# Two products of an MLP as seven quadrant products instead of eight, on one Trainium2 core

## The chip, the cores and the metric

The program runs on one core of one Trainium2 chip. The core has five engines with a queue of instructions each: TensorE (PE in the profile; its weight loads are listed as PEld), VectorE (DVE), ScalarE (ACT), GpSimd (POOL) and SyncE (SP), which here only issues DMAs. Each engine works through its queue in program order; semaphores make one engine wait for another. The metric is the time of one execution in microseconds of device time; lower is better. The kernel before takes 1270.71 us (median of 3 runs, 1268.05 to 1270.95).

## The reference

One layer of an encoder for 1024 prompt tokens and 32 sample tokens, model width 1024, in fp32. The change touches only the MLP at its end (`D_FF` is 4096):

```python
def trunk_layer(x, c, s0, ...):
    ...
    x = layer_norm(DN_ALPHA * x + (1.0 + gate1) * (mix @ w_o + b_o), ln1_g, ln1_b)
    h2 = x * (1.0 + scale2) + shift2
    f = jnp.square(jax.nn.relu(h2 @ w_up + b_up)) @ w_down + b_down
    x = layer_norm(DN_ALPHA * x + (1.0 + gate2) * f, ln2_g, ln2_b)
    return x, s_fin, v_rows
```

## The kernel before

**Tokens and precision.** The 1056 tokens stand in three blocks (`BLK`): blocks 0 and 1 have 384 tokens, block 2 has 288 (256 prompt, 32 sample). Activations are kept feature-major, 128 features by the tokens of a block. Every fp32 product is made from split operands: a value is a high part rounded to fp32r (a copy on ScalarE) and a low part (value minus high part, on VectorE, or on POOL for the activations), and three passes are multiplied, high by high, high by low, low by high (`PASS`). So one output tile of 128 features, summed over 1024 inputs, is 8 k-tiles by 3 passes, 24 matmuls.

**Weights.** `Units` (L146) takes the weights as units of 128 x 1024 (512 KB) in the order of their use, `main_units`: SP loads up to five ahead into `wst`, and two halves each are split into `whl` (L139 on ScalarE, L140 on VectorE), three units ahead. The list runs through all phases of the program without a break.

**Phase C/D.** After the mixers comes the output projection of each block (`out_proj`, matmuls at L251), the first layer norm on token-major rows (`norm1`: transposes at L1005 and L229, statistics, then h2 split by ScalarE and POOL, L238 and L241), and the MLP. For the layer norm the rows of x are loaded again (`xr`, L1021) with the gain row `ging` (L1013) and multiplied (`x_rows`, L1028 on VectorE for block 0, L1030 on ScalarE and L1031 on POOL for the others).

**The MLP** goes through the 32 feature tiles of f in eight groups of four. `up` (L251 for its matmuls) makes one tile for all three blocks: 24 matmuls per block, then relu with the bias (L1070, ScalarE), the square (L1071, VectorE), and the split of f (L1072, L1073). `down` (L1096) takes one weight unit, a pair of output tiles, and sums over the four tiles of the group: 12 matmuls per output tile and block, and adds them with the gate to the accumulator `acc` in SBUF (L1101). In the loop of `main_d`, the down pairs of group g and the up tiles of group g+1 alternate. The last group's down product is taken in pieces of tokens (`down_last`, L1159), each followed by the second layer norm of its rows (`norm2`).

**What sets the order.** The generators are woven by `Order`, which emits TensorE's work of the main stream and puts the other streams' pieces between by estimated times; the order of each engine's queue is the order of emission. PSUM has eight banks for output tiles in this phase (`mm()`).

Of the kernel before, what the change touches and what calls it, by code (L numbers as in the profile page):

```python
# [19 lines left out]
P = 128  # L20
# [16 lines left out]
# columns of the packed per-feature vectors  # L37
# [8 lines left out]
# weight units, each [128, 1024]  # L46
# [51 lines left out]
def build(tc, io):  # L98
# [4 lines left out]
    with ctx:  # L103
# [4 lines left out]
        wp = ctx.enter_context(tc.tile_pool(name="wp", bufs=1))  # L108
# [33 lines left out]
        class Units:  # L142
            """Weight units in the order of their use: loaded and split ahead of it."""

            def __init__(self, us):
                self.us, self.raw, self.hl, self.i = us, [], [], 0  # L146
                self.last, self.split = None, {}

            def ahead(self, nl, ns):
                while len(self.raw) < min(nl, len(self.us)) or len(self.hl) < min(ns, len(self.us)):  # L150
# [4 lines left out]
                    else:  # L155
                        if self.last and len(self.hl) == len(self.us) - 1:
                            hl = self.last()
                        else:
                            hl = wp.tile([P, 2, 1088], F32R, tag="whl", name="whl", bufs=3)
# [3 lines left out]
            def get(self, u, n=1):  # L163
                """the next n units, split; every use of the earlier ones has been emitted"""
# [60 lines left out]
        def turn(tiles, b, k):  # L225
            """token-major tiles of a block -> [128 features of tile k, tokens] in PSUM"""
# [5 lines left out]
        def split_affine(dst, pt, k, b, av, cv, tmp):  # L232
            """dst (hi, lo) = av * pt + cv"""
# [10 lines left out]
        PASS = ((0, 0), (0, 1), (1, 0))  # L244

        def fm_mm(pt, hl, act, n, korder, done):
            """[128 out features, n tokens]; hl holds 8 k-tiles of [128, 128]"""
            ks = list(korder)
            for i, k in enumerate(ks):
                for j, (a, b_) in enumerate(PASS):  # L250
                    PE.matmul(pt[:, :n], hl[:, a, 128 * k:128 * k + 128], act[:, b_, k, :n],  # L251
                              start=(i == 0 and j == 0), stop=(i == 7 and j == 2))
# [10 lines left out]
        def stack_s(pool, tag, bufs, wide=1):  # L263
            """the sample tokens, hi and lo rows side by side"""
# [4 lines left out]
        def tm_part(pt, hls, act, off, n, width, ks, passes=PASS):  # L269
            """[n tokens, width]; hls are the units that hold the k-tiles in order"""  # L270
# [22 lines left out]
        def proj_act(u0, ms, func, pool, tag, alloc=mm, ready=None):  # L293
            for m in ms:
                hl = wu.get(u0 + m)
                for b in range(3):
# [4 lines left out]
                    def done(pt):  # L301
# [8 lines left out]
        # ================= phase A: input layer norm, gMLP =================  # L310
        main_units = ([U_ZU + m for m in range(4)] + [U_R + m for m in range(4)]
                      + [U_V, U_V + 1, U_K, U_Q, U_K + 1, U_Q + 1, U_V + 2, U_V + 3]
                      + [U_O + m for m in range(8)] * 3 + [U_UP + m for m in range(4)])
        for g in range(7):
            main_units += [U_DN + 4 * g, U_UP + 4 * g + 4, U_DN + 4 * g + 1, U_UP + 4 * g + 5,
                           U_DN + 4 * g + 2, U_DN + 4 * g + 3, U_UP + 4 * g + 6, U_UP + 4 * g + 7]
        main_units += [U_DN + 28 + dp for dp in range(4)]
# [675 lines left out]
        with tc.tile_pool(name="pd", bufs=1, reuse_waits="tile") as pd, \  # L993
# [86 lines left out]
            def up(m, fs):  # L1080
                hl = wu.get(U_UP + m)
                f = new_f()
                for b in range(3):
                    yield from up_tile(hl, m, f, b)
# [222 lines left out]
```

## Time and profile before

| what | value |
|---|---|
| median of 3 runs | 1270.71 us (1268.05 to 1270.95) |
| span of the profiled execution | 1268.7 us |
| TensorE busy | 1217.2 us, 96% |
| VectorE busy | 728.5 us, 57% |
| ScalarE busy | 439.7 us, 35% |
| POOL busy | 246.6 us, 19% |
| moved from and to HBM | 94.29 MB read, 4.65 MB written |

The profile is of one execution; the page gives its span, from the first to the last instruction. It is 2.0 us under the median of the runs, and inside their spread. "Busy" of TensorE counts pipelined matmuls. A row of the grouped views reads: line, engine, operation, tiles written and read, shapes, count, then total busy time and the mean in ns of one, then the engine's idle time just before such instructions and what ended it. In a timeline or a chain, a row begins with its start and its length in us. Line numbers in rows of the profile before are those of the kernel printed above; those of the changed kernel are named as such.

### The profile page before, as it was taken

To read this page: it belongs to the slowest core of one execution; us is meant where nothing else is said; L and a number is where in the kernel's file an instruction comes from. 1 tells how busy PE (TensorE), PEld (TensorE's weight loads), DVE (VectorE), ACT (ScalarE), POOL (GpSimd) and SP (SyncE) were. 2 spreads that over 40 slices of the span, in tenths; PEclk is the share of its full clock that TensorE was granted. 3 is DMA by queue.
4 is the path that set the end of the run, shared out by engine and by line. 5 is a ranking of instruction groups with operands and counts; after the bars stand their busy time and mean duration, and the time that the engine had idled before them with its cause. 6 is when DMAs were issued, how large, how long until landed. Compare 5 with 4: busy or idle time off the path is not lost.

```text
span 1268.7 us, 21648 instructions
## 1 busy us (share of the span) xinstructions
PE 1217.2 (96%) x8779; PEld 1166.3 (92%) x8779; DVE 728.5 (57%) x1654; ACT 439.7 (35%) x960; POOL 246.6 (19%) x435
## 2 busy tenths in 40 slices
PE   5999996999899999999999999999999999999996
PEld 3689996988788899999999999999999999999996
DVE  5763999578886789644334434443344344344467
ACT  4463322445566666622122122221222221212311
POOL 3441232345584235200000000000000000000034
PEclk9999998899899999999999999999999999999998
DMA  9503555110002633020111111101111111111112
GB/s 373 205 2 130 177 221 183 34 35 19 22 35 72 236 134 117 9 75 36 49 50 51 34 51 50 51 34 51 51 50 34 50 51 49 36 51 50 67 38 100
DMA packets 29396, 100.34 MB, mean 79 GB/s; under 512 B 3408, under 2 KB 4912, under 8 KB 29296
## 3 DMA queue, kind: packets, MB, share of 16 engines
q1 hardware_dynamic: 29296, 98.95, 22.1%
q8 instruction: 69, 1.13, 0.4%
q14 instruction: 31, 0.25, 0.1%
HBM read 94.29 MB, written 4.65 MB: 78 GB/s over the span
## 4 chain that ended last, share of the span: by engine, by line
PE 81%; DVE 10%; DMA 4%; ACT 2%; issue 2%; POOL 1%; SPq 0%; DVEq 0%; ACTq 0%
PE mm L251 40%; PE mm L1096 26%; PE mm L1159 3%; PE zp L285 2%; DMA wst<-in_w_dram 2%; DVE jk L888 2%; PE mm L285 2%; DVE whl L140 1%; DVE wad L888 1%; PE mm L229 1%; PE zp L251 1%; DMA wad<-in_w_dram 1%; PE mm L1005 1%; PE gt L768 1%; DVE zx L746 1%
## 5 line engine op out<-in xcount | busy, mean ns | idle before, releaser
L251 PE MATMUL mm<-h,whl 128*128 128x384 f32 (+1 forms) x2304 | 377.1, 322 | 0.0
L251 PEld LDWEIGHTS mm<-h,whl 128*128 128x128 f32 x2304 | 370.7, 188 | 0.3
L1096 PE MATMUL mm<-f,whl 128*128 128x384 f32 (+1 forms) x2016 | 328.9, 323 | 0.0
L1096 PEld LDWEIGHTS mm<-f,whl 128*128 128x128 f32 x2016 | 326.7, 188 | 0.0
L139 ACT CAST whl<-wst 128x512 fp32r<-128x512 f32 x202 | 115.0, 618 | 283.0 <-PE mm L1096 203.9
L1101 DVE SCALAR_TENSOR_TENSOR acc<-mm,G,acc 128x384 f32<-128x384 f32 (+1 forms) x224 | 105.0, 490 | 168.6 <-PE mm L1096 168.6
L1071 DVE TENSOR_TENSOR rl<-rl 128x384 f32<-128x384 f32 (+1 forms) x96 | 50.7, 528 | 193.7 <-ACT rl L1070 193.7
L140 DVE TENSOR_TENSOR whl<-wst,whl 128x512 fp32r<-128x512 f32 x202 | 147.6, 766 | 17.0 <-ACT whl L139 14.3
L219 POOL TENSOR_SCALAR rs<-mv 128x1 f32<-128x1 f32 (+1 forms) x27 | 7.7, 285 | 756.0 <-DVE mv L218 756.0
L251 PE MATMUL mm<-hT,whl 128*128 128x384 f32 (+1 forms) x792 | 129.6, 322 | 1.0 <-ACT mix L307 1.0
L251 PEld LDWEIGHTS mm<-hT,whl 128*128 128x128 f32 x792 | 127.0, 188 | 2.6 <-ACT mix L307 1.6
L1070 ACT ACTIVATE rl<-mm,pv 128x384 f32<-128x384 f32 (+1 forms) x96 | 53.3, 555 | 202.0 <-PE mm L251 202.0
L251 PE MATMUL mm<-mhl,whl 128*128 128x384 f32 (+1 forms) x576 | 100.7, 329 | 3.0 <-DVE whl L140 3.0
L251 PEld LDWEIGHTS mm<-mhl,whl 128*128 128x128 f32 x576 | 93.2, 191 | 3.6 <-DVE whl L140 3.3
L1073 DVE TENSOR_TENSOR f<-rl,f 128x384 fp32r<-128x384 f32 (+1 forms) x96 | 50.7, 529 | 36.7 <-ACT f L1072 36.7
L285 PE MATMUL mm<-whl,hT 128*128 128x272 f32 (+1 forms) x384 | 58.1, 317 | 7.9 <-DVE whl L624 6.4
L285 PEld LDWEIGHTS mm<-whl,hT 128*128 128x128 f32 x384 | 55.8, 220 | 10.2 <-DVE whl L624 6.6
L1072 ACT CAST f<-rl 128x384 fp32r<-128x384 f32 (+1 forms) x96 | 46.8, 488 | 38.8 <-DVE rl L1071 38.8
L285 PE MATMUL zp<-zvw,hT 128*128 128x512 f32 x192 | 52.1, 416 | 4.5 <-ACT hT L238 4.5
L888 DVE SCALAR_TENSOR_TENSOR jk<-wad,csb 128x1024 f32<-128x1024 f32 x32 | 53.0, 1655 | 4.6 <-ACT csb L874 2.7
L285 PEld LDWEIGHTS zp<-zvw,hT 128*128 128x128 f32 x192 | 35.6, 195 | 14.9 <-ACT hT L238 6.7
L884 POOL TENSOR_TENSOR wad<-wad,csb 128x1024 f32<-128x1024 f32 x11 | 30.2, 2745 | 86.0 <-DVE jk L888 46.4
(209 smaller groups left out, 1249.0 us busy)
## 6 DMA issues: line engine op xcount, KB each, us to landing
wst<-in_w_dram SPq DMA_DIRECT2D x114, 512.0 KB, 3.5
wad<-in_w_dram SPq DMA_DIRECT2D x32, 512.0 KB, 4.3
st<-in_w_dram SPq DMA_DIRECT2D x10, 512.0 KB, 10.2
x<-in_x_dram SPq DMA_DIRECT2D x8, 512.0 KB, 7.9
xr<-in_x_dram SPq DMA_DIRECT2D x6, 512.0 KB, 9.3
out_dram<-row SPq DMA_DIRECT2D x6, 512.0 KB, 2.6
csb<-in_c_dram SPq DMA_DIRECT2D x2, 512.0 KB, 5.1
row<-in_x_dram SPq DMA_DIRECT2D x2, 512.0 KB, 9.1
```

The costliest lines, as they stand in the source:

```text
L139: S.copy(hl[:, 0, r], st[:, r])
L140: V.tensor_tensor(hl[:, 1, r], st[:, r], hl[:, 0, r].bitcast(F32), ALU.subtract)
L251: PE.matmul(pt[:, :n], hl[:, a, 128 * k:128 * k + 128], act[:, b_, k, :n], start=(i == 0 and j == 0), stop=(i == 7 and j == 2))
L285: PE.matmul(pt[:n, :width], act[:, a, k, off:off + n], hl[:, b_, width * kk:width * kk + width], start=(k == 0 and a + b_ == 0), stop=(k = ...
L888: V.scalar_tensor_tensor(jk, w, 1.0, csb[:, c], ALU.mult, ALU.mult, accum_out=acc_)
L1070: S.activation(t[:, :n], pt[:, :n], AF.Relu, bias=col("b_up", m))
L1071: V.tensor_tensor(t[:, :n], t[:, :n], t[:, :n], ALU.mult)
L1072: S.copy(f[:, 0, s0:s0 + n], t[:, :n])
L1073: V.tensor_tensor(f[:, 1, s0:s0 + n], t[:, :n], f[:, 0, s0:s0 + n].bitcast(F32), ALU.subtract)
L1096: PE.matmul(pt[:, :n], hl[:, a, o_:o_ + 128], fs[kk][:, c_, s0:s0 + n], start=(kk == 0 and j == 0), stop=(kk == 3 and j == 2))
L1101: V.scalar_tensor_tensor(ac, pt[:, off:off + w], G2[:, m, c:c + 1], ac, ALU.mult, ALU.add)
L1159: PE.matmul(pt[:, :n], hl[:, a, o_:o_ + 128], fs[kk][:, c_, s0:s0 + n], start=(kk == 0 and j == 0), stop=(kk == 3 and j == 2))
```

## The change

**The seven products.** For blocks 0 and 1 together (768 tokens), the up product of groups 1 to 7 and the down product of groups 1 to 6 are made by the Strassen-Winograd scheme. The operands are cut into quadrants, weights A11 to A22 and activations B11 to B22 (half of the inputs by one block). Seven products of quadrants or of sums of them replace eight. An up product of a group is then 7 x 2 x 12 = 168 matmuls of 384 columns instead of 192, and a down product as well. Block 2, group 0 and the down product of group 7 stay as they were.

**Sums of the inputs.** h2 is the same for all groups, so `t_prod` makes its sums T1 to T4 once, during group 0 (POOL adds and subtracts, ScalarE and VectorE split), and stores them with three plain quadrants in 14 DRAM tiles of 786 KB (`td`). Each of the seven groups loads all 14 again, by DMAs that POOL issues (L1291 of the changed kernel), into a ring of eight slots. The sums of the weights are made for each group on POOL (`_sums`, L1059 to L1062), in place in the loaded tiles, and split like the others: 32 half units per group instead of 16 whole ones in two halves. The sums of F, the activation between the two products, are made per group on VectorE (L1305, L1306) and POOL (L1308, L1310) and split (L1313 on ScalarE, L1314 on VectorE) into slots of the same ring.

**Output sums.** Winograd's partial sums stay in PSUM where two products can be added there, and otherwise go through `tmps` in SBUF. The evictions are longer for that: per group 16 operations of 384 columns on VectorE for up (L1352, L1353, L1360) and 36 for down (L1412, L1415, L1423).

**Memory and order.** The phase has its own weight store now, `Weights` (five raw slots, eleven split half units), in the pool `pd`; the old pool `wp` is closed before `pd` is opened, and `main_units` ends with the first output projection. So the loads of the second and third projection's weights are no longer part of the list that runs through.

SP's queue at the end of the mixers; the rows are DMAs, destination and source. Before (`wst` are weights; their last rows ahead of `ging` belong to the second output projection):

```order
L818 DMA out_dram<-st_1151 64x128 x2
L153 DMA wst<-in_w_dram 128x1024
L818 DMA out_dram<-st_1152 64x128 x2
L153 DMA wst<-in_w_dram 128x1024 x2
L1013 DMA ging<-in_ln_in_g_dram 128x1024
L1021 DMA xr<-in_x_dram 128x1024 x2
L1021 DMA row<-in_x_dram 128x1024
```

After (`raw` are the slots of the new store; the first one is lent to the gain row):

```order
L154 DMA wst<-in_w_dram 128x1024 x5
L813 DMA out_dram<-st_1151 64x128 x2
L813 DMA out_dram<-st_1152 64x128 x2
L1124 DMA raw<-in_ln_in_g_dram 128x1024
L1132 DMA xr<-in_x_dram 128x1024 x8
L1132 DMA xr<-in_x_dram 32x1024
L1071 DMA raw<-in_w_dram 128x1024 x12
```

The weights of the second projection moved from ahead of the gain row and of x to behind all nine loads of x. The gain row itself waits for the last matmul of the first output projection, whose operands lay where it goes; before, it waited for an earlier one.

VectorE's queue where a group passes from up to down. Before, in the loop of the MLP (splits of weights, two up tiles, adds of a down pair):

```order
L140 TENSOR_TENSOR whl<-wst,whl 128x512 x2
L1071 TENSOR_TENSOR rl<-rl 128x384
L1073 TENSOR_TENSOR f<-rl,f 128x384
L1071 TENSOR_TENSOR rl<-rl 128x384
L1073 TENSOR_TENSOR f<-rl,f 128x384
L1071 TENSOR_TENSOR rl<-rl 128x288
L140 TENSOR_TENSOR whl<-wst,whl 128x512 x2
L1073 TENSOR_TENSOR f<-rl,f 128x288
L1101 SCALAR_TENSOR_TENSOR acc_5384<-mm,G_1158,acc_5384 128x384 x2
```

After, from the last eviction of an up product on (L1216 adds block 2's down tiles; L1305 and L1306 make T2 of F; the last row's neighbours of the same line are splits of other tiles):

```order
L1352 SCALAR_TENSOR_TENSOR tmps<-mm,pv,tmps 128x384
L1015 TENSOR_TENSOR hl<-raw,hl 128x512
L1216 SCALAR_TENSOR_TENSOR acc_6161<-mm,G_1158,acc_6161 128x256
L1353 SCALAR_TENSOR_TENSOR F<-tmps 128x384
L1216 SCALAR_TENSOR_TENSOR acc_6161<-mm,G_1158,acc_6161 128x32
L1216 SCALAR_TENSOR_TENSOR acc_6161<-mm,G_1158,acc_6161 128x256
L1305 TENSOR_TENSOR F<-F 128x2x384
L1216 SCALAR_TENSOR_TENSOR acc_6161<-mm,G_1158,acc_6161 128x32
L1306 TENSOR_TENSOR F<-F 128x2x384
L1216 SCALAR_TENSOR_TENSOR acc_6161<-mm,G_1158,acc_6161 128x256
L1216 SCALAR_TENSOR_TENSOR acc_6161<-mm,G_1158,acc_6161 128x32
L1314 TENSOR_TENSOR ring<-F,ring 128x768
```

Behind these rows stand a weight split, two more adds of block 2, and the split of T2 (L1314), for which the second product of down waits. What was a short row of independent evictions is now a chain whose end TensorE needs.

POOL's queue at the same place; before, POOL has nothing in the loop of the MLP. After (L1060 waits for the L1015 row above, L1308 for L1306):

```order
L1059 TENSOR_TENSOR raw<-raw 128x512
L1291 DMA ring<-tdB_5124 128x1536
L1060 TENSOR_TENSOR raw<-raw 128x512
L1061 TENSOR_TENSOR raw<-raw 128x512
L1062 TENSOR_TENSOR raw<-raw 128x512
L1308 TENSOR_TENSOR F<-F 128x2x384
L1310 TENSOR_TENSOR F<-F 128x2x384
L1059 TENSOR_TENSOR raw<-raw 128x512
```

Three sums of weights and two of F have come to stand beside VectorE's chain.

The core of the diff (lines that only lost a comment are left out):

```diff
+        wctx.close()
         with tc.tile_pool(name="pd", bufs=1, reuse_waits="tile") as pd, \
...
+            raw_t = pd.tile([P, 5, 1024], F32, name="raw")
+            hl_t = pd.tile([P, 11, 2, 512], F32R, name="hl")
...
+                def _sums(self, key):
+                    u1, u2, s = self.raw[*key, 1], self.raw[*key, 2], halves.take()
+                    a11, a12, a21, a22 = u1[:, :512], u1[:, 512:], u2[:, :512], u2[:, 512:]
+                    self.raw[*key, 0] = s
+                    G.tensor_tensor(s, a21, a22, ALU.add)
+                    G.tensor_tensor(a21, a11, a21, ALU.subtract)
+                    G.tensor_tensor(a11, s, a11, ALU.subtract)
+                    G.tensor_tensor(a12, a12, a11, ALU.subtract)
...
+            SEQ = (("P1", "A11", "B11", 0, True), ("P6", "S2", "T2", 1, True), ("P2", "A12", "B21", 0, False),
+                   ("P7", "S3", "T3", 1, False), ("P5", "S1", "T1", 2, True), ("P4", "A22", "T4", 1, False),
+                   ("P3", "S4", "B22", 2, False))
+            td = {(t, j): dr.tile([P, 1536], F32, name=f"td{t}{j}") for _, _, t, _, _ in SEQ for j in range(2)}
...
+                    for _, _, t, _, _ in SEQ:
+                        for j in range(2):
+                            ring.queue.append((("t", self.g, t, j), lambda: True, lambda s, t=t, j=j:
+                                               G.dma_start(s, td[t, j].rearrange("p (a c) -> p a c", a=2))))
...
+                def f_split(self, t, s):
+                    f11, f12, f21, f22 = (self.f[:, 2 * i:2 * i + 2, 384 * j:384 * j + 384] for i in range(2) for j in range(2))
+                    if t == "T2":
+                        V.tensor_tensor(f12, f22, f12, ALU.subtract)
+                        V.tensor_tensor(f11, f12, f11, ALU.add)
+                    elif t == "T1":
+                        G.tensor_tensor(f22, f22, f11, ALU.subtract)
+                    elif t == "T4":
+                        G.tensor_tensor(f21, f21, f11, ALU.subtract)
+                    src = {"B11": f11, "B22": f22, "B21": f21, "T2": f11, "T3": f12, "T1": f22, "T4": f21}[t]
+                    q = quad(s)
+                    S.copy(q[:, 0], src)
+                    V.tensor_tensor(q[:, 1], src, q[:, 0].bitcast(F32), ALU.subtract)
...
+                        for prod, a_, t, s, first in SEQ:
+                            f = quad(ring.get("f", g, t))
+                            hl = W.get("d", g, r, a_)
+                            for q in range(2):
+                                if first:
+                                    self.sums[s][q] = mm()
+                                pt = self.sums[s][q]
+                                for kk in range(2):
+                                    for i, (a, b_) in enumerate(PASS):
+                                        o_ = 256 * kk + 128 * q
+                                        PE.matmul(pt[:, :384], hl[:, a, o_:o_ + 128], f[:, b_, kk],
+                                                  start=first and kk + i == 0, stop=kk + i == 3,
+                                                  skip_group_check=True)
+                                self.down_up(prod, q, 2 * r + q)
```

More of the change, by code (lines that the diff above doesn't have):

```diff
@@ L155, in ahead @@
                     else:
[L156 to L159, printed above, removed]
+                        hl = wp.tile([P, 2, 1088], F32R, tag="whl", name="whl", bufs=3)
                         self.split.get(self.us[len(self.hl)], split)(hl, self.raw[len(self.hl)])
@@ L1007, in to_rows @@
                 return pts
-            def row():
-                return pd.tile([P, D], F32, tag="row", name="row", bufs=4)
-            ging = pd.tile([P, 2, D], F32, tag="f", name="ging", bufs=6)[:, 0]
+            ging = raws.take()
             DM.dma_start(ging, io["ln_in_g"].to_broadcast([P, D]))
@@ L1031, in x_rows @@
                         G.tensor_tensor(t[:n], t[:n], ging[:n], ALU.mult)
+                if b == 2:
+                    raws.give(ging)
             def norm1(b):
@@ L1063, in norm1, with tmp_tile, out_proj_d, up_std @@
                 h2[b], acc[b] = h2b, accb
-            def up_tile(hl, m, f, b):
-                s0, n = BLK[b]
+            def tmp_tile(name):
+                return pd.tile([P, 384], F32, tag="tmp", name=name, bufs=3)
+            def out_proj_d(b):
+                yield lambda: y[b] is not None
+                for m in range(KT):
+                    yield from fm_tile(W.unit_of("o", b, m), mhl[b], BLK[b][1], out_done(b, m), KO)
+                    W.unit_done("o", b, m)
+            def up_std(hl, m, b, f):
+                n = BLK[b][1]
@@ new lines, in build, with __init__, pump, get @@
+            class Ring:
+                def __init__(self, aps):
+                    self.slots, self.queue, self.out = Slots(aps), [], {}
+                def pump(self):
+                    while self.queue and self.slots.free:
+                        key, ready, make = self.queue[0]
+                        if not ready():
+                            break
+                        self.queue.pop(0)
+                        self.out[key] = self.slots.take()
+                        make(self.out[key])
+                def get(self, *key):
+                    self.pump()
+                    return self.out[key]
+                def done(self, *key):
+                    self.slots.give(self.out.pop(key))
+                    self.pump()
@@ new lines, in main_d @@
+                hl = [W.unit_of("u", 0, m) for m in range(2)]
+                for m in range(2):
+                    yield from up_std(hl[m], m, 0, fa(m, 0))
+                yield lambda: h2[1] is not None
+                f_a.append(pd.tile([P, 2, 2, 768], F32R, tag="R", name="f", bufs=2))
+                for m in range(2):
+                    yield from up_std(hl[m], m, 1, fa(m, 1))
+                yield lambda: h2[2] is not None
+                fb2 = pd.tile([P, 4, 2, 288], F32R, tag="R", name="fb2", bufs=2)
@@ new lines, in main_d @@
+                for m in range(4):
+                    if m > 1:
+                        hl.append(W.unit_of("u", 0, m))
+                        for b in range(2):
+                            yield from up_std(hl[m], m, b, fa(m, b))
+                    yield from up_std(hl[m], m, 2, fb2[:, m])
+                    W.unit_done("u", 0, m)
+                yield lambda: tp not in order.streams
+                ring_t = [actp.tile([P, 4, 2, 768], F32R, tag=f"act{b}", name="ring") for b in range(2)]
@@ new lines, in main_d @@
+                ring = Ring([t[:, i] for t in ring_t for i in range(4)])
+                groups = [Group(g) for g in range(8)]
+                for gr in groups[1:]:
+                    gr.queue()
+                ring.pump()
+                for i in range(4):
+                    hl = W.unit_of("d", 0, i)
+                    for b in range(3):
+                        for q in range(2):
+                            pt = mm()
+                            n = BLK[b][1]
+                            down_mm(pt, hl, q, lambda kk: fb2[:, kk] if b == 2 else fa(kk, b), n)
+                            down_ev(pt, 4 * (i % 2) + 2 * (i // 2) + q, ((b, 0, n),))
+                            yield 12 * cost(n), 0
+                    W.unit_done("d", 0, i)
@@ L1202, in main_d @@
+                tmps_t = pd.tile([P, 8, 384], F32, tag="R", name="tmps", bufs=2)
+                tmps = Slots([tmps_t[:, i] for i in range(8)])
+                for g in range(1, 7):
+                    yield from groups[g].up()
+                    yield from groups[g].down()
+                yield from groups[7].up()
+                ring.pump()
+                rows_.extend(raws.free)
+                l2.append(pd.tile([P, 2, D], F32, tag="F", name="l2", bufs=1))
                 for j, n in enumerate("gb"):
```

381 lines of the change are left out of this document (289 added, 92 removed).

## The prediction

> **What bounds the kernel now.** I read the page first (busy time, chain), then a table of windows over the MLP, then the chain of waits inside one group of the MLP. The page:
>
> ```profile
> span 1268.7 us, 21648 instructions
> ...
> PE 1217.2 (96%) x8779; PEld 1166.3 (92%) x8779; DVE 728.5 (57%) x1654; ACT 439.7 (35%) x960; POOL 246.6 (19%) x435
> ...
> PE 81%; DVE 10%; DMA 4%; ACT 2%; issue 2%; POOL 1%; SPq 0%; DVEq 0%; ACTq 0%
> ```
>
> TensorE is busy for 96% of the span and is 81% of the chain that ends last. Where the change acts, the MLP, it is more than that. The table of windows (busy us of each engine, granted clock, DMA share, GB/s) and the chain across two periods of the loop:
>
> ```profile
> 560.00:1180.00 620.00, 620.00 (x3859) 620.00 (x3859) 250.96 (x485) 137.45 (x264) 0.00 (x0) 1.00 0.14 46
> ```
>
> ```profile
> 552.61 11.63 PE mm L1096 x72
> 564.24 11.54 PE mm L251 x72
> 575.79 11.63 PE mm L1096 x72
> 587.42 11.54 PE mm L251 x72
> 598.97 23.24 PE mm L1096 x144
> 622.21 23.02 PE mm L251 x144
> 645.23 4.92 PE mm L1096 x28
> ```
>
> In 620 us TensorE never idles, at full clock (1.00); VectorE is busy for 40%, ScalarE for 22%, POOL for nothing, and 46 GB/s are moved. One group (four down pairs, four up tiles, 576 matmuls) lasts 645.23 - 552.61 = **92.62 us**. So here a removed matmul is removed time, until another engine takes over.
>
> **What the change removes.** A matmul of 384 columns: 30 in 5.25 us and 6 in 1.05 us, both 0.175 us, in the chain around the boundary of the phases:
>
> ```profile
> 406.66 5.25 PE mm L251 x30
> ...
> 414.89 5.30 DMA ging<-in_ln_in_g_dram
> ...
> 420.25 12.41 DMA wst<-in_w_dram
> ...
> 443.60 3.34 PE mm L251 x10
> 446.94 0.33 PE mm L229 x3
> 447.27 1.05 PE mm L251 x6
> ```
>
> A tile of 72 matmuls is 48 of these and 24 of 288 columns: (11.54 - 8.40) / 24 = 0.131 us each. The up products of groups 1 to 7 on blocks 0 and 1 were 7 x 192 = 1344 matmuls and become 7 x 168 = 1176; the down products of groups 1 to 6 were 1152 and become 1008. That is 312 fewer, 312 x 0.175 = **-54.6 us**: 8.4 in each of groups 1 to 6 (92.6 to 84.2), 4.2 in group 7, whose down product stays.
>
> **The boundary into the MLP phase.** The weights of the second and third output projection come from a new pool now, whose memory comes free only when the first projection's last matmul is done. SP sends the gain row `ging`, then the nine loads of `x`, and only then the first weight; before, weights had been split three units ahead, and TensorE went straight on:
>
> ```profile
> 415.18 5.50 PE L251 MATMUL mm<-mhl,whl 128*128 128x384 f32 x30
> 420.52 1.25 PE L1005 MATMUL mm<-ident,y 128*128 128x128 f32 x8
> 421.53 2.70 PE L251 MATMUL mm<-mhl,whl 128*128 128x384 f32 x14
> ```
>
> ```profile
> 421.00:424.00 3.00, 3.00 (x20) 2.76 (x18) 2.31 (x3) 1.42 (x3) 0.00 (x0) 1.00 1.03 423
> 424.00:427.00 3.00, 3.00 (x22) 2.97 (x21) 3.00 (x5) 1.30 (x2) 0.00 (x0) 1.00 1.03 411
> ```
>
> `ging` can now leave at about 420.5. Ahead of and with the first weight, 0.52 + 8.25 x 0.52 + 0.52 = 5.4 MB are moved; at the 411 GB/s of the second row that is 13.1 us, with some 2 us until such a stream is up. First weight at 435.5, cast 0.6 and subtraction 0.7, some waiting for POOL (below): TensorE resumes near 437.5, **16 us** later than now. Queued behind that wait is all of TensorE's work. What it gives back: the stall of 2.99 us at 440.6 before, which the chain shows as a weight load that left behind `x` (420.25, 12.41 us), since the first five units then have landed. Net **+13**; bounds +8 (loads at once at 423 GB/s, no engine waiting) and +18 (two casts more queued ahead on ScalarE and VectorE).
>
> **The third block's h2.** Up tiles of blocks 0 and 1 cover its normalization. Before, three weight units (144 matmuls) do so, now two (96), 8.4 us less; five of its eight turns stand back to back ahead of its first product, which needs POOL's low part of every turn, behind POOL's new input sums.
>
> ```profile
> 518.64 0.81 POOL L241 TENSOR_TENSOR h<-t,h 128x288 fp32r<-128x288 f32 x1 [5.32 <-ACT h L238]
> 520.15 0.80 POOL L241 TENSOR_TENSOR h<-t,h 128x288 fp32r<-128x288 f32 x1 [0.71 <-ACT h L238]
> ```
>
> One turn takes 1.5 us there; five are 7.5 us, of which the product itself (24 x 0.131 = 3.1) runs alongside: 4.4, plus POOL's queue: **+5**, bounds 0 and +10. The input sums (32 POOL operations of 384 columns at about 1.07 us, 34 us) are not needed before group 1, behind four units of group 0 (some 90 us): nothing, unless POOL's order pushes them under this wait, which the bound holds.
>
> **The groups.** New work per group: VectorE and ScalarE split 32 half units instead of 16, seven operand tiles of F (768 columns), the eviction chains; POOL makes 16 weight sums of 512 columns and 2 sums of F, and sends 14 loads of 0.79 MB. The groups by line that price them:
>
> ```profile
> L140 DVE TENSOR_TENSOR whl<-wst,whl 128x512 fp32r<-128x512 f32 x108 | 69.9, 688 | 1.9
> L1101 DVE SCALAR_TENSOR_TENSOR acc<-mm,G,acc 128x384 f32<-128x384 f32 x109 | 67.2, 616 | 112.0 <-PE mm L1096 112.0
> L1101 DVE SCALAR_TENSOR_TENSOR acc<-mm,G,acc 128x256 f32<-128x256 f32 x56 | 27.1, 484 | 54.2 <-PE mm L1096 54.2
> L1101 DVE SCALAR_TENSOR_TENSOR acc<-mm,G,acc 128x32 f32<-128x32 f32 x56 | 13.6, 242 | 0.0
> L1071 DVE TENSOR_TENSOR rl<-rl 128x288 f32<-128x288 f32 x26 | 11.9, 458 | 36.7 <-ACT rl L1070 36.7
> L1073 DVE TENSOR_TENSOR f<-rl,f 128x288 fp32r<-128x288 f32 x26 | 11.7, 451 | 0.0
> L624 DVE TENSOR_TENSOR whl<-wst,whl 128x1024 fp32r<-128x1024 f32 x2 | 2.4, 1214 | 0.0
> L241 POOL TENSOR_TENSOR h<-t,h 128x384 fp32r<-128x384 f32 x16 | 17.0, 1074 | 13.2 <-ACT h L238 13.1
> L1116 POOL TENSOR_TENSOR row<-row,l 128x1024 f32<-128x1024 f32 x6 | 14.4, 2401 | 7.3 <-DVE row L1115 7.3
> ```
>
> On lines through these, VectorE needs 0.95 us for 768 columns, POOL about 1.3 for 512 and 1.85 for 768. VectorE's sum per group: 32 x 0.69 splits, 9 x 0.95 for F, 52 evictions x 0.62, and for block 2 eight times 0.73 and four times 0.91: 72 of 84 us. That fits, so the loss lies in single waits. The one that I can follow is the passage from up to down. The second product there needs the low part of T2, the end of a chain on VectorE: last up eviction, two sums of F, two splits. TensorE has four tiles of block 2 (48 x 0.131 = 6.3) and one product (12 x 0.175 = 2.1), so it wants T2 0.2 us into the next, **8.7 us** after up's last matmul. VectorE's queue in that stretch, in the order of the new program: 0.62, 0.69, (wait for a block-2 tile, until 1.6) 0.48, 0.62, 0.24, (until 3.2) 0.48, 0.95, 0.24, 0.95, 0.48, 0.24, 0.95, 0.69, 0.48, 0.24, 0.95. It ends at 9.9: 1.2 us late, 7 us in six groups. But POOL's sums L1060 to L1062, L1308 and L1310 fall into the same stretch, and the trace shows what that does (timeline at the boundary):
>
> ```profile
> 435.39 0.67 DVE L140 TENSOR_TENSOR whl<-wst,whl 128x512 fp32r<-128x512 f32 x1
> ...
> 437.83 5.16 POOL L1031 TENSOR_TENSOR xr<-xr,ging 128x1024 f32<-128x1024 f32 x2
> ...
> 439.35 7.58 DVE L140 TENSOR_TENSOR whl<-wst,whl 128x512 fp32r<-128x512 f32 x4 [1.24 <-ACT whl L139]
> ...
> 442.96 2.81 POOL L1031 TENSOR_TENSOR row<-row,ging 128x1024 f32<-128x1024 f32 x1
> 443.60 3.02 PEld L251 LDWEIGHTS mm<-mhl,whl 128*128 128x128 f32 x10 [3.31 <-DVE whl L140]
> 443.60 3.34 PE L251 MATMUL mm<-mhl,whl 128*128 128x384 f32 x10 [2.99 <-DVE whl L140]
> ```
>
> A split that takes 0.67 us alone takes 1.9 on average (four in 7.58) while POOL multiplies: the engines take turns, each waiting for the other's whole operation. Replayed so, VectorE's two-input operations wait: L1353 ends at 3.2, L1305 at 5.5, L1306 at 7.7, the next split at 10.5, a weight split at 13.0, T2's low part at **14.7**: 6.0 us late. After 2.99 us of idleness ten matmuls took 3.34 us at 443.60 instead of 1.75, so 1.6 more is lost: **7.6 us per group**, 45.6 in six. Bounds: 7 (no turns taken) and 54 (one more turn of 1.3 us each). I take 45.6, because the row that shows two such streams side by side is this one.
>
> The Trainium skill ("SBUF — State Buffer", section "SBUF: two separate sides") states this as a rule: a VectorE operation with two SBUF inputs and a GpSimd operation that reads SBUF exclude each other for the whole instruction. The four splits in 7.58 us agree; without the rule the sum would end near 1241, with it near 1280.
>
> No row shows a load that POOL sends; the nearest is SP's of 512 KB, 3.5 us to landing in the page's table of DMA issues:
>
> ```profile
> wst<-in_w_dram SPq DMA_DIRECT2D x114, 512.0 KB, 3.5
> ```
>
> The ring lets the new loads leave 12.6 us before their use (rival 3), so I cost them at nothing; if POOL's queue holds them up by more than that leaves, rival 3 has the price.
>
> **The sum.** -54.6 + 13 + 5 + 45.6 = **+9.0 us**. The trace's span is 1268.7 and the runs are 1268.05 to 1270.95, so what lies around the span is within the spread of the runs; on the median of 1270.7 it makes **1280**. The tail keeps its pieces and row work: nothing.
>
> **Rivals.**
> 1. *The turns are not taken, or fall elsewhere* (faster). If POOL's five sums are done before up ends, or stand behind T2, the passage costs 1.2 instead of 7.6 us: 1280 - 38 = **1241**, with the boundary's lower bound 1236. For it: VectorE is at 40% now, and operations reading PSUM need not wait. It decides at 8.7 us: T2 ready by then, and each group keeps its 8.4. Against it: the sums become ready with the split that stands ahead of the chain.
> 2. *VectorE becomes the bound* (slower). 72 us of its own and 16 x 1.3 + 2 x 1.85 = 24.5 us of POOL, fully excluding each other, are 96.5 us per group: six times 12.3 more than 84.2, so 1270.7 - 54.6 + 18 + 74 = **1308**. Against it: only some 42 of the 72 us have two SBUF inputs, and 42 + 24.5 stays under 84.
> 3. *The input sums arrive late* (slower). An up product takes 24 x 0.175 = 4.2 us and reads 1.57 MB; four products are in the ring, the fifth's loads leave when the first ends, 12.6 us ahead, and need 3.8 us at 411 GB/s (3.5 for 0.5 MB by the row above, 5 or so by that pace). A lag of over 7.6 us in POOL's queue makes a wait; 5 us a group on top give **1310**.
>
> **Chances and range.** Forecast 0.50, rival 1 0.28, rival 2 0.14, rival 3 0.08. The forecast's own range is 1264 to 1298: its bounds at the boundary (5 us each way), the h2 wait (5) and the passage (8 up, the low end with two of six passages on time). The range is **1238 to 1304**: it takes in rival 1 but for its last bound, and the lower half of rivals 2 and 3, so that under 2 in 10 is left out. By 0.3% (3.8 us, about what a measurement of this kernel can tell from none): faster 0.34 (rival 1 and a low edge of the forecast), same 0.14, slower 0.52.
>
> **What the new profile would show.** Boundary: a TensorE idle stretch of some 16 us after the first output projection, ended by the first `raw` split. Groups: a period of 91.8 us instead of 92.6, with one idle time of about 6 us before the second product of each down (released by VectorE, line 1314), granted clock below 1.00 there, and two-input VectorE operations of 1.3 us and more beside POOL's. If the period is 85 to 86, the turns don't matter and rival 1 holds; if VectorE is above 95% busy in the groups, rival 2; if TensorE waits for `ring` loads, rival 3. I am wrong outright if TensorE idles at other places of the group, in the eviction waits of the down product for example, which I have counted at nothing since VectorE there has 72 of 84 us.

## The result, and the profile after

The changed kernel takes **1312.41 us** (median of 4 runs, 1307.65 to 1315.84), the kernel before beside it 1270.83: ratio 1.0337, 95% interval 1.0308 to 1.0366. That is 41.6 us slower, where 9 were forecast; the direction was right, the time lies 8 us above the range of 1238 to 1304. The profiled execution's span grew from 1268.7 to 1310.6 us, by 41.9.

The first lines of the page:

```profile
span 1310.6 us, 22153 instructions
...
PE 1185.9 (90%) x8467; PEld 1129.3 (86%) x8467; DVE 976.6 (75%) x1952; ACT 525.1 (40%) x1080; POOL 515.9 (39%) x681
```

The 312 matmuls are gone (8779 to 8467), but TensorE's busy time fell by only 31.3 us, since part of the rest ran at a lower clock, and its share fell from 96% to 90%. One group of the MLP in the table of windows (busy us of PE, PEld, DVE, ACT, POOL, then granted clock, DMA share and GB/s):

```profile
831.25:927.33 96.08, 86.55 (x531) 85.83 (x529) 73.00 (x117) 32.84 (x57) 34.71 (x33) 0.95 0.46 159
```

VectorE is busy for 73.0 us of 96.1, about what the prediction summed (72), and TensorE for 86.6. The table of TensorE's waits, without those that were there before (us in all, times, longest):

```profile
PE mm L1397 <- DVE ring L1314: 29.7, 6, 5.0
PE mm L250 <- ACT hl L1014: 17.8, 1, 17.8
PE mm L1397 <- ACT ring L1313: 17.8, 6, 4.8
...
PE mm L1119 <- ACT y L936: 6.8, 4, 3.1
...
PE mm L250 <- POOL h L239: 1.8, 4, 0.6
```

Six waits of each kind on L1397 are one per group, and they are the only waits in the groups: TensorE's rows of one passage from up to down show that both stand at one place, the second down product.

```profile
736.20 29.29 PE L1337 MATMUL mm<-ring,hl 128*128 128x384 f32 x168
765.33 6.54 PE L1205 MATMUL mm<-fb,hl 128*128 128x288 f32 x48
771.70 2.28 PE L1397 MATMUL mm<-ring,hl 128*128 128x384 f32 x12
777.26 0.44 PE L1397 MATMUL mm<-ring,hl 128*128 128x384 f32 x1 [3.27 <-ACT ring L1313]
782.73 14.92 PE L1397 MATMUL mm<-ring,hl 128*128 128x384 f32 x71 [5.03 <-DVE ring L1314]
```

Block 2 and the first product follow up without a gap; then comes a wait for the high part of T2 (cast by ScalarE, L1313), one matmul, and a wait for the low part (VectorE, L1314). The first wait was not in the forecast. Between the starts of up's products in the first and in the seventh group (642.10 and 1210.18) lie 568.1 us: a **period of 94.7 us**, against 92.6 before and 91.8 forecast. Rows of VectorE and POOL from the timeline there:

```profile
768.84 0.62 DVE L1352 SCALAR_TENSOR_TENSOR tmps<-mm,pv,tmps 128x384 f32<-128x384 f32 x1
769.37 1.26 DVE L1015 TENSOR_TENSOR hl<-raw,hl 128x512 fp32r<-128x512 f32 x1
...
770.72 1.28 POOL L1060 TENSOR_TENSOR raw<-raw 128x512 f32<-128x512 f32 x1
770.95 1.48 DVE L1353 SCALAR_TENSOR_TENSOR F<-tmps 128x384 f32<-128x384 f32 x1
...
772.08 1.49 POOL L1061 TENSOR_TENSOR raw<-raw 128x512 f32<-128x512 f32 x1
...
772.90 1.49 DVE L1305 TENSOR_TENSOR F<-F 128x768 f32<-128x768 f32 x1
773.65 1.86 POOL L1062 TENSOR_TENSOR raw<-raw 128x512 f32<-128x512 f32 x1
...
774.48 1.86 DVE L1306 TENSOR_TENSOR F<-F 128x768 f32<-128x768 f32 x1
...
776.42 1.81 POOL L1308 TENSOR_TENSOR F<-F 128x768 f32<-128x768 f32 x1 [0.90 <-DVE F L1306]
776.81 2.23 DVE L1314 TENSOR_TENSOR ring<-F,ring 128x768 fp32r<-128x768 f32 x1
...
778.19 2.52 POOL L1310 TENSOR_TENSOR F<-F 128x768 f32<-128x768 f32 x1
...
778.97 2.29 DVE L1015 TENSOR_TENSOR hl<-raw,hl 128x512 fp32r<-128x512 f32 x1
...
781.74 0.94 DVE L1314 TENSOR_TENSOR ring<-F,ring 128x768 fp32r<-128x768 f32 x1
```

The engines take turns as forecast: an operation of 768 columns that takes 0.94 us alone (last row) takes 1.49, 1.86 and 2.23 beside POOL, and POOL's of 1.28 takes 1.49 and 1.86. But up's last matmul ends near 765.4, and VectorE's first row of this chain starts at 768.84: it had 3.5 us of work left from before. Where that backlog begins, some 11 us earlier, the rows show a wait of another kind:

```profile
752.55 1.28 POOL L1059 TENSOR_TENSOR raw<-raw 128x512 f32<-128x512 f32 x1 [2.87 <-DMA raw<-in_w_dram]
...
755.88 1.28 POOL L1061 TENSOR_TENSOR raw<-raw 128x512 f32<-128x512 f32 x1
757.19 1.66 ACT L1014 CAST hl<-raw 128x512 fp32r<-128x512 f32 x3 [4.31 <-PE mm L1337]
...
757.85 1.23 DVE L1015 TENSOR_TENSOR hl<-raw,hl 128x512 fp32r<-128x512 f32 x1 [2.73 <-ACT hl L1014]
```

VectorE stood idle for 2.73 us, because the next split in its queue waited for a cast, and the cast for the sum that L1061 makes for the first half of down's weights, which ended at 757.16 (the profile names TensorE for the cast's own wait, but the cast starts 0.03 us behind L1061). POOL in turn had waited 2.87 us for a load (L1059) ahead of that sum. This is a wait for data, not a turn. The six groups bear it out: L1061 ended 18.0 us after up's start in one of them, 20.4 to 21.0 in four and 22.2 in one; TensorE's first wait there was 0.9, 2.7 to 3.3 and 4.8 us, while its second was 4.8 to 5.0 in all six.

At the boundary:

```profile
423.17 1.25 PE L1119 MATMUL mm<-ident,y 128*128 128x128 f32 x8
442.21 6.51 PE L250 MATMUL mm<-mhl,hl 128*128 128x384 f32 x24 [17.79 <-ACT hl L1014]
```

After 17.79 us of idleness the first 24 matmuls take 6.51 us instead of 4.2 (granted clock 0.65 from 442.0 to 448.5).

Where the 41.9 us of the span lie, by three marks of TensorE (start of the transposes behind the first projection, of the first down product, of the last one):

| stretch | before, us | after, us | difference | forecast |
|---|---|---|---|---|
| start to the first projection's end | 420.52 | 423.17 | +2.7 | 0 |
| to the first down product | 132.09 | 159.93 | +27.8 | +18 |
| to the last down product | 648.18 | 656.21 | +8.0 | -9.0 |
| to the end | 67.95 | 71.29 | +3.3 | 0 |

### The profile page after: what moved, and what is told of

It reads as the page before. It is cut to its first block, busy times and chain, and to the rows that moved or that the text cites. A ratio compares the mean times of both kernels' runs of the same rounds, so it can differ in the third digit from the quotient of the medians.

```text
span 1310.6 us, 22153 instructions
## 1 busy us (share of the span) xinstructions
PE 1185.9 (90%) x8467; PEld 1129.3 (86%) x8467; DVE 976.6 (75%) x1952; ACT 525.1 (40%) x1080; POOL 515.9 (39%) x681
## 4 chain that ended last, share of the span: by engine, by line
PE 41%; DVE 10%; issue 2%; POOL 1%; DMA 1%; ACT 1%; DVEq 0%; POOLq 0%; ACTq 0%
PE mm L1397 13%; PE mm L1205 9%; PE mm L1337 9%; PE mm L250 9%; DVE hl L1015 3%; DVE F L1353 2%; DVE tmps L1352 1%; DMA raw<-in_w_dram 1%; DVE acc L1216 1%; DVE ring L1314 1%; DVE F L1305 1%; ACT hl L1014 1%; POOL raw L1060 0%; DVE F L1306 0%; PE mm L1119 0%
## 5 line engine op out<-in xcount | busy, mean ns | idle before, releaser
L1015 DVE TENSOR_TENSOR hl<-raw,hl 128x512 fp32r<-128x512 f32 (+1 forms) x280 | 237.5, 853 | 91.4 <-ACT hl L1014 90.4
L1014 ACT CAST hl<-raw 128x512 fp32r<-128x512 f32 (+1 forms) x280 | 168.4, 614 | 298.1 <-PE mm L1397 129.5
L1397 PE MATMUL mm<-ring,hl 128*128 128x384 f32 x1008 | 194.6, 354 | 47.4 <-DVE ring L1314 29.7
L1397 PEld LDWEIGHTS mm<-ring,hl 128*128 128x128 f32 x1008 | 188.6, 201 | 51.2 <-DVE ring L1314 31.5
L1337 PE MATMUL mm<-ring,hl 128*128 128x384 f32 x1176 | 205.0, 334 | 0.0
L1337 PEld LDWEIGHTS mm<-ring,hl 128*128 128x128 f32 x1176 | 203.7, 188 | 0.0
L250 PE MATMUL mm<-h,hl 128*128 128x288 f32 (+1 forms) x960 | 144.1, 309 | 2.0 <-POOL h L239 1.8
L250 PEld LDWEIGHTS mm<-h,hl 128*128 128x128 f32 x960 | 139.5, 192 | 3.7 <-POOL h L239 2.7
L1059 POOL TENSOR_TENSOR raw<-raw 128x512 f32<-128x512 f32 x26 | 37.6, 1448 | 235.6 <-DMA raw<-in_w_dram 94.2
L1205 PE MATMUL mm<-fb,hl 128*128 128x288 f32 x768 | 104.8, 295 | 0.0
L1205 PEld LDWEIGHTS mm<-fb,hl 128*128 128x128 f32 x768 | 103.7, 188 | 0.0
L250 PE MATMUL mm<-mhl,hl 128*128 128x384 f32 (+1 forms) x384 | 67.2, 331 | 17.8 <-ACT hl L1014 17.8
L1216 DVE SCALAR_TENSOR_TENSOR acc<-mm,G,acc 128x256 f32<-128x256 f32 (+3 forms) x176 | 62.2, 388 | 14.9 <-PE mm L1205 14.8
L1313 ACT CAST ring<-F 128x768 fp32r<-128x768 f32 x42 | 35.1, 835 | 84.5 <-DVE F L1305 39.2
L1291 POOL DMA_DIRECT2D ring<-tdT x56 | 30.6, 547 | 94.8 <-PE mm L1337 51.0
```

Source lines behind the costliest of these rows:

```text
L250: PE.matmul(pt[:, :n], h[:, a, 128 * kk:128 * kk + 128], act[:, b_, k, :n], start=(i == 0 and j == 0), stop=(i == 7 and j == 2))
L1014: S.copy(hl[:, 0, :n], src)
L1015: V.tensor_tensor(hl[:, 1, :n], src, hl[:, 0, :n].bitcast(F32), ALU.subtract)
L1059: G.tensor_tensor(s, a21, a22, ALU.add)
L1205: PE.matmul(pt[:, :n], hl[kk // 2][:, a, o_:o_ + 128], f(kk)[:, c_], start=(kk == 0 and j == 0), stop=(kk == 3 and j == 2))
L1216: V.scalar_tensor_tensor(ac, pt[:, o + lo - p0:o + hi - p0], G2[:, m, c:c + 1], ac, ALU.mult, ALU.add)
```

## The experiments

Ten runs, each with the kernel before on the same chip. Ratios are to it, with 95% intervals.

**The boundary.** Three weight units go ahead of the gain row and of x:

```diff
             ging = raws.take()
+            W.pump()
             DM.dma_start(ging, io["ln_in_g"].to_broadcast([P, D]))
```

> The first three weight units of the second output projection are loaded ahead of the gain row and of x; nothing else changes. If TensorE's 17.8 us of idleness after the first projection are the wait for weights that stand behind x: 1.6 MB arrive in about 6 us, so the idle time falls to 7 to 9 us, and the whole to 1300 to 1304 us. If x is what is needed first (the norm of block 0 becomes late in turn), the idle time moves to a later place and the whole stays within 1309 to 1313.

Measured: 1300.48 us, ratio 1.0260 (1.0224 to 1.0296). TensorE's waits between the first projection and the first down product in that run:

```profile
PE mm L1119 <- ACT y L936: 5.9, 2, 3.1
PE mm L250 <- DVE hl L1015: 3.9, 2, 3.0
PE mm L250 <- ACT hl L1014: 3.8, 1, 3.8
```

The wait of 17.8 us became 3.8, less than the 7 to 9 expected; 3.9 came back later, most of it (3.0) at a split that runs beside POOL's products of x. From the first projection's end to the first down product it takes 149.2 us instead of 159.9, 10.7 less. So the place of the loads in SP's queue made the wait, as forecast.

**Which engine makes T2 late.** Three runs take POOL's operations away from the passage, in part and then all but one. First, three of the four weight sums are left out:

```diff
                     G.tensor_tensor(s, a21, a22, ALU.add)
-                    G.tensor_tensor(a21, a11, a21, ALU.subtract)
-                    G.tensor_tensor(a11, s, a11, ALU.subtract)
-                    G.tensor_tensor(a12, a12, a11, ALU.subtract)
```

> Leaves out three of the four weight sums that POOL makes (L1060 to L1062); the first sum and the sums of F stay on POOL. If VectorE's two-input operations wait for POOL's running operation: the chain to T2's low part is shorter by what L1353, L1305 and L1306 lose in the trace (0.9 + 0.5 + 0.9 us) and a little more, the two waits of TensorE before the second down product fall from 8.3 to about 5.5 us a group, the whole to 1290 to 1297. If the chain is late by VectorE's own work alone: waits of 8 us, the whole at 1308 or above.

Then POOL's two sums of F go to VectorE, behind T2's split:

```diff
                     elif t == "T1":
-                        G.tensor_tensor(f22, f22, f11, ALU.subtract)
+                        with tc.issue_after(self.t2):
+                            V.tensor_tensor(f22, f22, f11, ALU.subtract)
                     elif t == "T4":
-                        G.tensor_tensor(f21, f21, f11, ALU.subtract)
+                        with tc.issue_after(self.t2):
+                            V.tensor_tensor(f21, f21, f11, ALU.subtract)
...
-                    V.tensor_tensor(q[:, 1], src, q[:, 0].bitcast(F32), ALU.subtract)
+                    lo = V.tensor_tensor(q[:, 1], src, q[:, 0].bitcast(F32), ALU.subtract)
+                    if t == "T2":
+                        self.t2 = lo.ins
```

> The two sums of F that POOL makes are made on VectorE instead, issued behind the split of T2; the weight sums stay on POOL. If the engines exclude each other: T2's low part comes 2.9 us earlier (L1314 and L1015 lose 1.3 and 1.6 us beside POOL in the trace), the waits fall from 8.3 to 5 to 6 us, VectorE has 1.9 us more per group behind it; the whole 1293 to 1300. If not: no earlier, and 1.9 us more on the busier engine, 1312 to 1322.

And both edits together:

> Both: three of four weight sums left out, and the sums of F on VectorE. If the engines exclude each other, no POOL operation but the first weight sum is left beside the chain, which loses 5.8 us in the trace by the lengths of its operations: waits of 2 to 3 us per group, period 86 to 88 us instead of 94.7, the whole 1262 to 1274. If VectorE's own queue makes the chain late: waits of over 6 us, the whole over 1300.

| | time, us | ratio | period, us | waits for T2, six groups, us |
|---|---|---|---|---|
| as changed | 1312.41 | 1.0337 (1.0308 to 1.0366) | 94.7 | 47.5 |
| three weight sums left out | 1281.88 | 1.0096 (1.0070 to 1.0123) | 89.4 | 20.7 |
| sums of F on VectorE | 1297.25 | 1.0217 (1.0180 to 1.0255) | 92.2 | 32.9 |
| both | 1249.34 | 0.9840 (0.9810 to 0.9870) | 84.6 | 2.6 |

The last one is the clear answer, and gained more than expected. Its passage (the same program places as above, with other line numbers: L1353 here is L1352 above, L1302 and L1303 are L1305 and L1306, L1313 is L1314, L1398 is L1397):

```profile
755.06 6.54 PE L1202 MATMUL mm<-fb,hl 128*128 128x288 f32 x48
...
755.67 0.61 DVE L1353 SCALAR_TENSOR_TENSOR tmps<-mm,pv,tmps 128x384 f32<-128x384 f32 x1
...
758.86 0.95 DVE L1302 TENSOR_TENSOR F<-F 128x768 f32<-128x768 f32 x1
...
759.89 0.95 DVE L1303 TENSOR_TENSOR F<-F 128x768 f32<-128x768 f32 x1
...
763.33 0.95 DVE L1313 TENSOR_TENSOR ring<-F,ring 128x768 fp32r<-128x768 f32 x1
...
764.33 3.92 PE L1398 MATMUL mm<-ring,hl 128*128 128x384 f32 x21 [0.44 <-DVE ring L1313]
```

With those POOL operations away every VectorE operation of the chain has its own length, but for one split beside the weight sum that is left (1.25 us). The chain starts 0.6 us after up's end and not 3.5, it lasts 8.6 us and not 13.8, T2 comes 9.2 us after up's end and not 17.4, and the wait is 0.44 us. So of the 8.1 us by which T2 was late, 5.2 are turns taken beside the chain and 2.9 the backlog ahead of it. VectorE's own work is not the cause: it is the same work, and 1.9 us more per group.

The two runs before it separate the parts. Without the three weight sums the cast no longer waits for L1061: the chain starts 0.6 us after up's end, the first wait is gone, and the second is 3.5 us per group. That gained more than expected (period 89.4 instead of some 92). With only the sums of F moved the backlog stays: the chain starts 3.7 us after up's end, the first wait keeps its size (20.3 us in six groups), and the second falls from 29.7 to 12.6.

**Reading or only running.** The run with both edits once more, with POOL busy at the same places by operations that read nothing from SBUF:

```diff
                     G.tensor_tensor(s, a21, a22, ALU.add)
-                    G.tensor_tensor(a21, a11, a21, ALU.subtract)
-                    G.tensor_tensor(a11, s, a11, ALU.subtract)
-                    G.tensor_tensor(a12, a12, a11, ALU.subtract)
+                    for a_ in (a21, a11, a12):
+                        for _ in range(2):
+                            G.memset(a_, 0.5)
```

> As the run without POOL's operations at the chain (1249 us, period 84.6 us), but in place of the three weight sums left out POOL writes constants to the same three places, twice each: POOL operations that write SBUF and read none. It leaves out the same three weight sums. If VectorE waits only for POOL operations that read SBUF: period 84.6 us, the whole 1246 to 1254. If any running POOL operation holds it: six operations of some 0.5 us beside the chain, period 86.5 to 88, the whole 1260 to 1270.

Measured: 1251.09 us, ratio 0.9865 (0.9839 to 0.9891), period 84.6 to 85.1. At its passage:

```profile
757.19 1.66 POOL L1059 TENSOR_TENSOR raw<-raw 128x512 f32<-128x512 f32 x1 [1.25 <-DMA raw<-in_w_dram]
...
758.15 1.25 DVE L1015 TENSOR_TENSOR hl<-raw,hl 128x512 fp32r<-128x512 f32 x1
...
759.82 1.59 POOL L1062 MEMSET raw<- 128x512 f32 x3
...
760.80 0.95 DVE L1305 TENSOR_TENSOR F<-F 128x768 f32<-128x768 f32 x1
```

The split beside POOL's sum takes 1.25 us; the sum of F beside POOL's writes of constants takes 0.95, its own length. So a busy POOL does not hold VectorE; one that reads SBUF does. (The weight splits wait for these writes as they did for the sums, but the writes take 0.53 us each; no idle time like that of 2.73 us stands in VectorE's rows ahead of this passage.) The Trainium skill ("SBUF — State Buffer", section "SBUF: two separate sides") names this condition, a GpSimd operation that reads SBUF against a VectorE operation with two SBUF inputs, and the two rows agree with it.

**All sums on VectorE.**

```diff
-                    G.tensor_tensor(s, a21, a22, ALU.add)
+                    V.tensor_tensor(s, a21, a22, ALU.add)
```

and so for the other three, with the two edits of the first and the third run.

> All weight sums and the sums of F on VectorE, and the three weight units ahead of x as in the first run: POOL has nothing left in the groups but its loads. VectorE had 67.1 us of 84.6 in a group of the run without POOL's operations; 13 more sums of 0.69 us make 76. If only POOL's operations beside the chain cost time: period 85 to 87 us, the whole 1235 to 1250. If VectorE now runs late by itself (the second rival of the prediction): period 90 or more, the whole over 1270.

Measured: 1284.08 us, ratio 1.0125 (1.0104 to 1.0147), period 91.3: a miss. VectorE is not at its limit, as the window of one group shows (busy us of PE, PEld, DVE, ACT, POOL):

```profile
816.08:907.90 91.82, 86.74 (x531) 86.16 (x530) 73.79 (x136) 33.35 (x57) 7.54 (x14) 0.96 0.47 166
```

73.79 of 91.82 us. TensorE waits at the same place as in the changed kernel (16.6 us for T2's high part, 12.8 for its low part): in a passage looked at, the chain starts 4.4 us after up's end and lasts 9.8 us, with three weight sums between its rows and others ahead of it. What counts is what stands ahead of T2 in that queue, on whichever engine it runs.

**Only the sums beside the chain.** POOL keeps the sums of up's weights and of the first half of down's. The second half's, which fell into the passage, go to VectorE, issued behind T2, as do the sums of F; weights ahead of x. The core of the edit:

```diff
+                    if key[0] == "d" and key[2] == 1:
+                        with tc.issue_after(t2[key[1]]):
+                            V.tensor_tensor(s, a21, a22, ALU.add)
+                            V.tensor_tensor(a21, a11, a21, ALU.subtract)
+                            V.tensor_tensor(a11, s, a11, ALU.subtract)
+                            V.tensor_tensor(a12, a12, a11, ALU.subtract)
+                        return
                     G.tensor_tensor(s, a21, a22, ALU.add)
```

> POOL keeps its sums of up's weights and of the first half of down's weights; the sums that fell beside the chain (the second half of down's weights, the sums of F) are made on VectorE, issued behind the split of T2; three weight units ahead of x. If only what stands beside the chain counts: period 85 to 87 us, the whole 1238 to 1252, faster than the kernel before. If POOL's other sums hold VectorE as much somewhere else: period over 90 us, the whole over 1270.

Measured: **1246.86 us, ratio 0.9844** (0.9825 to 0.9863), faster than the kernel before, with nothing left out. One group, and the larger of the two kinds of waits in six groups (the other, for evictions, is 1.7 us in all):

```profile
885.33:971.00 85.67, 84.73 (x531) 83.82 (x530) 71.93 (x123) 33.48 (x57) 24.83 (x27) 1.00 0.50 179
```

```profile
PE mm L1411 <- DVE ring L1326: 2.9, 6, 0.7
```

POOL is busy for 24.83 us of this group, against 34.71 in one of the changed kernel, and costs about 1 us (84.6 without its operations). It still stretches VectorE's operations elsewhere (a split takes 1.30 us at 732.75), but TensorE waits for none of them. The sums of the first half come earlier as well. In the changed kernel a sum of the second half (L1059 at 752.55) stood ahead of three of them in POOL's queue and waited for its load; with it gone from there, the first of these three starts 14.0 us after up's start instead of 17.6, and VectorE has no backlog (the chain starts 0.6 us after up's end).

**Seven products for up alone.** Down of every group by eight products, block 2 of all four pairs first; weights ahead of x. The edit of the weight list:

```diff
-                if g < 7:
-                    for r in range(2):
-                        W.bundle((("d", g, r), (d + 2 * r, d + 2 * r + 1)))
-                else:
-                    for i in (0, 2, 1, 3):
-                        W.unit(("d", 7, i), d + i)
+                for i in (0, 2, 1, 3):
+                    W.unit(("d", g, i), d + i)
```

> Seven products for up alone; down of every group by eight, block 2 of all four pairs first; three weight units ahead of x; POOL keeps the weight sums of up. 24 matmuls of 0.174 us less per group than before, seven groups: 29 us. 12.7 us of block 2's down tiles cover four splits of F (some 6 us, 9 with POOL beside them), so no wait is expected: period 88.4 us, the whole 1258 to 1268. If the splits of F come late: a wait of over 2 us a group, the whole over 1275.

Measured: 1259.86 us, ratio 0.9934 (0.9913 to 0.9955), period 87.95, no wait in the groups. Up's half of the scheme gives 4.7 us of the 92.6 per group without loss, although POOL still makes 8 sums per group. (The 24 matmuls removed make 4.2; where the other 0.5 comes from was not traced.)

**A fourth slot.** The gain row is laid where weight sums come only later, so that the two projections have four raw slots (added to the run with the sums beside the chain on VectorE):

```diff
-            ging = raws.take()
+            ging = raw_t[:, 4]
...
-                if b == 2:
-                    raws.give(ging)
```

> As the run with the sums beside the chain on VectorE and three weight units ahead of x; the gain row now lies where weight sums come later, so the second and third projection have four raw slots for weights instead of three, and four units go ahead of x. There ScalarE waited 14.0 us for weights to land and TensorE some 15 us in all between the first projection and the first down product. If the third slot is what is short: half of these waits go, the whole 1236 to 1243. If the loads are bound by the splits that free the slots, or x comes too late: 1244 to 1250, as without.

> The kernel with the sums beside the chain on VectorE once more, beside the one with four slots on the same chip: 1244 to 1249.

Measured side by side: **1239.76 us, ratio 0.9746** (0.9721 to 0.9771) with four slots, 1247.58, ratio 0.9813 (0.9792 to 0.9833), without. From the first projection's end to the first down product it took 143.2 us with four slots and 152.4 without. ScalarE's waits for weights to land fell from 14.8 to 5.6 us, and TensorE's waits from 16.1 to 12.3: those for the evictions of `y` from 6.8 to 3.7, those for weight splits behind the first from 3.6 to none, and 2.7 us of waits at transposes came in. The slot was short, as expected, though less than half of TensorE's waits went. This is the fastest version found: all of the change, with the loads, four slots and the place of six sums altered.

## Why the prediction was right and wrong

- **The removed matmuls: right.** With the waits gone the period is 84.6 us, 8.0 below 92.6 (forecast 8.4; the other 0.4 is the last wait for T2).
- **Where the loss lies and the turns: right.** TensorE waits at the second product of down and nowhere else in the groups, VectorE's two-input operations take turns with POOL's, and the runs with POOL's operations moved or replaced show that as a cause. Counted from its first row the chain ran much as replayed: L1305 ended after 5.5 us (5.5 in the replay), L1306 after 7.5 (7.7), T2's low part after 13.8 (14.7). The measured time stands beside the figures of rivals 2 and 3 (1308 and 1310) by coincidence: no matmul waited for a load of the ring (rival 3), and VectorE was busy for 73.0 us of 96.1, not above 95% (rival 2).
- **The passage: the first step that failed.** The prediction let VectorE's chain begin with up's last matmul; a backlog ahead of it was put at nothing, without a reason. The chain began 3.5 us later, because VectorE's queue had stood for 2.73 us behind a split whose weight sum POOL had not yet made, and T2 came 17.4 us after up's end (782.68 against 765.33) instead of 14.7. The prediction had looked at POOL's sums of the second half only, and at the turns only; the sums of the first half cost by being late. It also left out TensorE's wait for T2's high part, 17.8 of the 47.5 us. So the term of 7.6 us per group measured 10.5 (94.7 less the 84.2 that the removed matmuls leave): 7.9 of waits, the rest at half clock (the next 71 matmuls took 14.92 us, and 12.59 in the run without POOL's operations). That is some 17 us more in six groups, and 9 beyond the bound of 54.
- **The boundary: too small, the second step that failed.** The wait was put at 16 us and was 17.8, and the stall of 3.0 was given back as forecast. But the wait costs clock, which the prediction charged in the groups and forgot here: 2.3 us in the first 24 matmuls. And it took the projections to run without waits once the first weights were there; four waits for `y` made 6.8 us, where before one made 2.0. ScalarE evicts `y` behind casts in its queue that wait for weights to land (15.3 us in all there), and the run with four slots shows that the slots were short. Together with the next term it is 27.8 us instead of 18: 21.6 of waits, and 6.2 for the same 818 matmuls at a lower clock.
- **The third block's h2: within its bounds.** 2.0 us of waits (1.8 for POOL, 0.2 for ScalarE), and a granted clock of 0.73 from 550 to 555 us, for a forecast of 5 with bounds 0 and 10.
- **The range: too narrow.** Its upper end of 1304 lies little above the forecast's own, 1298, which has the boundary, the h2 wait and the passage at their bounds (5, 5 and 8 more). The passage alone went 17 over, and the start and the end of the program, put at nothing, added 2.7 and 3.3. Two sums of the prediction don't quite come out, which changes nothing here: its 8.7 us add up to 8.6, and the low end of 1264 is lower by the terms that it names (5, 5 and two passages of 6.4 make 1257).
- **Not explained.** The start is 2.7 us longer; between runs with the same code there the first projection's end varies by more (420.65 to 424.60). At the end, 15.2 us lie between TensorE's end and that of the span, 10.4 before, and 15.2 again in all ten variants. The last operations on VectorE end at 1302.3 us and at 1265.5; what the rest waits for the rows don't show, and it wasn't tried. Why the load that POOL waited for ahead of the first half's sums came when it did was not traced either.

## What to carry to other kernels

Before work is moved to an idle engine, look for the chain that a bound engine waits for, and for what reads the same memory beside it: six POOL operations of 1.3 to 1.8 us each cost 9 us per group (a period of 94.7 us, and 85.7 with the same six on VectorE behind the chain). Part of that was turns taken beside the chain, part a sum that came late for a row ahead of it. A share of busy time hides both (VectorE was at 76%); replay the queue of the chain with the backlog it starts with, and ask of each row in it whose result it waits for. And when a pool is closed and another opened, look at what the load queue then sends first: a prefetch that ran across the boundary is lost without a line of the diff that names it.

## What the runs showed of the hardware

- POOL operations without an SBUF input (constants, 128 x 512, 0.53 us) leave VectorE's operations with two SBUF inputs at their length (0.95 us for 768 columns); a sum of two SBUF operands of the same size (1.28 us) holds them (1.49 and 1.86 us).
- Half clock came after short idle times too: the prediction's row after 2.99 us, and in the kernel before this one, after 2.01 us of waiting for `y`:

```profile
497.05 0.33 PE L1005 MATMUL mm<-ident,y 128*128 128x128 f32 x1 [2.01 <-ACT y L941]
...
497.46 2.04 PE L251 MATMUL mm<-h,whl 128*128 128x384 f32 x6
```

Six matmuls in 2.04 us are 0.34 each, twice the 0.175 of full clock; the granted clock is 1.00 from 493 to 495 us and 0.65 from 497.0 to 499.5. The Trainium skill ("TensorE: Matmul & The Clock Gate", section "What's actually happening") puts the drop after at least one idle window of about 3.4 us. Here 2.0 us of idle time was enough, and the measurement decides.

- POOL's loads of 768 KB (the 786 KB tiles, in units of 1024 bytes) took 6.8 us to landing (median of the changed kernel's page), SP's weight loads of 512 KB 4.0; issuing one held POOL for 0.55 us. No matmul waited for one of POOL's loads.
